# A third DMA-transposed unit in each attention layer, with two layouts on GpSimd, in a two-layer decoder trunk

## The chip, the cores and the metric

The kernel runs on one core of a Trainium2 chip. The metric is the device time of one execution in microseconds (us), lower is better. Several runs of the kernel are timed, and one more execution is recorded by the hardware profiler. In the profile PE is TensorE (PEld its weight loads), DVE is VectorE, ACT is ScalarE, POOL is GpSimd and SP is SyncE; a q behind a name (SPq) is that engine's queue of waits and DMA issues.

## What is computed

Two layers work on 512 tokens of width 1024 in float32. Each is a half-weighted SwiGLU feed-forward block, a mixing block, and a second feed-forward block. The mixing block has attention heads and a short convolution side by side:

```python
h = rms_norm(x, mix_norm[l])
z = h @ w_in[l]                      # q | k | v | conv_B | conv_C | conv_h
attn_out = sliding_window_attention(q, k, v, attn_sink[l])   # 8 heads, 2 kv heads, window 128
conv_out = short_conv(conv_B, conv_C, conv_h, conv_w[l])     # B * causal_conv3(C * h)
x = x + concat([attn_out, conv_out]) @ w_out[l]
```

In attention, a block of 128 queries sees its own 128 keys and the 128 before them (`k_band`, `v_band` below), with a bias by distance, a mask and a learned sink for each head:

```python
m = max(max(scores), sink)
p = where(mask, exp(scores - m), 0)
probs = p / (sum(p) + exp(sink - m))
out = probs @ v_band
```

## The kernel before

**Float32 by halves.** Every float32 operand is split into a high half, rounded to the format that TensorE reads (fp32r), and a low half with the remainder; a product is three matrix products (high x high, low x high, high x low). The high half of a weight (`wh`) is a cast on ScalarE, the low one (`wl`) a subtraction on VectorE (line 228). Weights come by SP from memory into buffers of the pool tag `raw`, of which there are eight; the attention tiles `p` and `vv` take buffers of the same tag.

**The mixing block.** `mix` (from about line 1482) first makes keys, values and four groups of queries. Then come twelve products of the convolution, two rounds of six (gate C twice, h twice, B twice). Attention is cut into eight units, `todo[0]` to `todo[7]`: index 0 to 3 are the four query blocks of the first key/value head, 4 to 7 those of the second. A unit holds four query heads. Index 2 is the third unit, index 3 the fourth. Units 0 and 4 are the first blocks of the sequence and have only one key block, the others two.

**Steps.** Attention is laid between the products by hand. Steps 2 to 5 follow the query groups, steps 6 to 17 the twelve products (product 9 is that of step 9). After each product `attend(step)` looks up in tables of steps which stages of which units are due:

- `scores` (table `SCORES_AT`): score products on TensorE, bias and maximum on VectorE (line 1558), exponentials on ScalarE (1575), scaling by the sum on VectorE (1583). The result `p` has queries on the partitions.
- `send` (table `SEND_AT`, step to unit): only for units 1, 3 and 5. A ScalarE copy (line 1590) lays the two 16-bit halves of all words of `p` apart into a room of the tile `crossing`, and SP issues a DMA transpose of the 16-bit rows back into the buffer of `p` (line 1592).
- `turn` (table `TURN_AT`): brings `p` to keys on the partitions. For a unit that was sent, `join` puts the turned halves together again with one ScalarE copy for each key block (line 1601). For the others TensorE transposes each head and key block into PSUM (line 1616). In both cases a ScalarE cast makes `ph` (1621) and a VectorE subtraction `pl` (1622).
- `values` (table `VALUES_AT`): two TensorE products for each key block (`ph`, line 1633; `pl`, line 1634), a ScalarE copy `ol` (1636) and two VectorE additions into `mixed[0]` (1639).

`INSIDE = (11, 4, 5)` puts the turn of unit 4 inside the product of step 11, in front of its sixth k. So `attend(10)` skips the turn that the table names for that step.

**What else runs in these steps.** In the h products (steps 8 and 9, and again 14 and 15) ScalarE makes two scaled copies, VectorE adds a tap (line 1712, both inputs in SBUF), and GpSimd does an addition and a multiplication (lines 1715 and 1716). The B products write `mixed[1]` (line 1720): its chunks 0 and 1 in steps 10 and 11, chunks 2 and 3 in steps 16 and 17.

**Order.** A scheduler at build time orders each engine's instructions, by the order of the program and by what it reckons is ready; the queues then run in that order. `issue_after` keeps the instructions of a block behind a given one on its engine. After a step, the next weights are split; if `attend` returns an instruction (the last `pl` of a turn, say), the low halves are ordered behind it. Joins are ordered behind the latest weight cast.

Of the kernel before, what the change touches and what calls it, by code (L numbers as in the profile page):

```python
# [54 lines left out]
STREAM_BACK_AT = {9: 0, 11: 1, 16: 2, 18: 3}  # L55
SCORES_AT = (5, 6, 7, 8, 9, 10, 12, 13)

SEND_AT = {7: 1, 9: 3, 11: 5}
TURN_AT = (6, 9, 8, 11, 10, 13, 14, 15)
VALUES_AT = (7, 10, 9, 12, 11, 14, 15, 16)  # L60
INSIDE = (11, 4, 5)
WARM = 3
XT_TAGS = ("sc", "aux", "aux", "mm", "sc", "sc", "aux", "aux")
# [12 lines left out]
def trunk_kernel(  # L76
# [23 lines left out]
    nc = tc.nc  # L100
# [11 lines left out]
    def g2(name, dt=F32, shape=(P, S)):  # L112
        return work.tile(list(shape), dt, tag="g2", bufs=14, name=name)

    def g8(name, dt=F32R, shape=(P, 2, 2, S)):
        return work.tile(list(shape), dt, tag="g8", bufs=4, name=name)
# [18 lines left out]
    def words(ap):  # L135

        return ap.bitcast(U16).rearrange("p (n two) -> p two n", two=2)
# [1356 lines left out]
    def mix(l, norm, after):  # L1494
        q = [None] * NH

        mixed = [g8(f"m_{l}_{j}", F32, (P, KC // 2, S)) for j in range(2)]
# [37 lines left out]
        class Unit:  # L1535
# [49 lines left out]
            def send(self):  # L1585


                self.room = crossing[:, todo.index(self) // 2 % 2, :]
                halves = self.room.bitcast(U16).rearrange("p (two n) -> p two n", two=2)
                nc.scalar.copy(halves, words(self.p.rearrange("p h k -> p (h k)")))  # L1590
                self.turned = self.p.rearrange("p h k -> p (h k)").bitcast(U16)
                nc.sync.dma_start_transpose(
                    self.turned.rearrange("p (c q) -> p c q", q=P),
                    halves.rearrange("p two n -> p (two n)"),
                )
# [11 lines left out]
            def turn(self):  # L1607

                self.pt = []
                for kb in range(self.lo // P, 2):  # L1610
                    if todo.index(self) in SEND_AT.values():
                        tp = self.join(kb)
# [30 lines left out]
        todo = [Unit(n, g) for g in range(NKV) for n in range(NT)]  # L1643
        crossing = g8(f"crossing_{l}", F32, (P, 2, 4 * 2 * P))

        def attend(step):

            done = None
            if step in SEND_AT:
                todo[SEND_AT[step]].send()  # L1650
            for at, stage in ((VALUES_AT, "values"), (TURN_AT, "turn"), (SCORES_AT, "scores")):
                if stage == "turn" and step + 1 == INSIDE[0]:
                    done = todo[VALUES_AT.index(step)].added
                    continue
                if step in at:
                    done = getattr(todo[at.index(step)], stage)() or done
            return done

        for j in range(NH // 2):
            acc = group(norm.h) if j else qacc  # L1660
            if j == 3:
                vv = take_values()
            qf = scaled(acc, f"qf_{l}_{j}", by=1.0 / 8.0)
            both = form(f"q_{l}_{j}", shape=(P, 2, S))
            qe, qo = both[:, 0, :], both[:, 1, :]
            nc.scalar.copy(qe[:HD, :], qf[:HD, :])
            nc.scalar.copy(qo[HD:, :], qf[HD:, :])
            nc.vector.tensor_sub(qe[HD:, :], qf[:HD, :], f32(qe[:HD, :]))
            nc.vector.tensor_sub(qo[:HD, :], qf[HD:, :], f32(qo[HD:, :]))
            q[2 * j], q[2 * j + 1] = qe, qo  # L1670
            attend(2 + j)
# [4 lines left out]
        step = 6  # L1676
# [9 lines left out]
        def go_on():  # L1686

            nonlocal step
            last = attend(step)
            if step == TURN_AT[-1]:  # L1690
                state["turned"] = last.ins
            step += 1
            with tc.issue_after(last.ins) if last else nullcontext():
                need_split(state["group"] - 1 + SPLIT_AHEAD + (step >= TURN_AT[-1]))

        for pair in range(2):
            cs = []
            for j in range(2):
                c = g2(f"cc_{l}_{pair}_{j}")
# [4 lines left out]
            for j in range(2):  # L1704
                c = 2 * pair + j
# [79 lines left out]
```

## Time and profile before

| what | us |
|---|---|
| median of 3 runs | 1626.99 |
| lowest and highest | 1626.08 and 1627.02 |
| the profiled execution, its own time | 1626.19 |
| its span, first to last instruction | 1624.4 |
| TensorE busy in the span | 1615.4 |
| VectorE, ScalarE, GpSimd busy | 1376.7, 1178.1, 216.5 |

The granted TensorE clock is 0.999 over the span. The steps 6 to 17 of layer 0 lie between 368 and 450 us, those of layer 1 between 1171 and 1253 us.

How to read the lines: a row of the timeline has start, duration, engine, line of the kernel, operation, output<-input, shape and count, and in brackets how long the engine was idle before it and what released it. A row of a source line has count, shortest/median/longest duration in ns, and first and last start. A row of a group has busy us and the mean of one in ns. Matrix products overlap in the pipeline, so their durations sum to more than their starts span.

### The profile page before, as it was taken

How to read it: one execution, taken by the hardware profiler on the slowest of the kernel's cores; microseconds unless marked ns; L12 is line 12 of the kernel's file. 1: busy time of each engine (PE TensorE's matmuls, PEld its weight loads, DVE VectorE, ACT ScalarE, POOL GpSimd, SP SyncE). 2: the span in 40 equal slices, each digit the busy share in tenths (PEclk: the TensorE clock that was granted, in tenths of full speed). 3: DMA queues.
4: the chain of work that ended last, by engine and by line, in shares of the span. 5: the costliest groups of instructions: out<-in, count | busy, mean ns of one | idle time of the engine just before them, and what ended most of it. 6: DMA issues, size and time to landing. Idle time of an engine off the chain costs nothing.

```text
span 1624.4 us, 21158 instructions
## 1 busy us (share of the span) xinstructions
PE 1615.4 (99%) x7571; PEld 1349.4 (83%) x7571; DVE 1376.7 (85%) x1788; ACT 1178.1 (73%) x1511; POOL 216.5 (13%) x191
## 2 busy tenths in 40 slices
PE   9999999999999999999999999999999999999998
PEld 7888888888898888888888888888888988888887
DVE  7978798988899977798998777989688998678997
ACT  6677777857766677778866777788586767878665
POOL 1211111001211111111011111110012111111121
PEclk9999999999999999999999999999999999999999
DMA  9999989822597698999767999998136978999892
GB/s 270 212 232 209 220 207 226 233 59 78 143 227 175 177 225 214 218 214 225 218 144 182 224 215 226 215 221 217 42 91 156 233 149 219 225 223 222 241 230 72
DMA packets 306031, 313.92 MB, mean 193 GB/s; under 512 B 125501, under 2 KB 188549, under 8 KB 305925
## 3 DMA queue, kind: packets, MB, share of 16 engines
q1 hardware_dynamic: 265412, 230.90, 50.1%
q0 software_dynamic: 40048, 81.27, 29.3%
q8 instruction: 59, 0.97, 0.2%
q14 instruction: 48, 0.39, 0.1%
q10 hardware_dynamic: 464, 0.40, 0.1%
HBM read 264.29 MB, written 2.10 MB: 164 GB/s over the span
## 4 chain that ended last, share of the span: by engine, by line
PE 98%; DVE 1%; DMA 0%; SPq 0%; issue 0%; ACT 0%; DVEq 0%
PE x L842 27%; PE y L842 13%; PE x_s L842 9%; PE acc L318 7%; PE acc L319 7%; PE acc L321 7%; PE w L842 7%; PE y_s L842 5%; PE x_m L827 3%; PE w_s L842 3%; PE y_m L827 1%; PE y_e L842 1%; PE acc L699 1%; PE x_e L842 1%; PE w_m L827 1%; PE sc L1555 0%
## 5 line engine op out<-in xcount | busy, mean ns | idle before, releaser
L228 DVE TENSOR_TENSOR wl<-raw,wh 128x1024 fp32r<-128x1024 f32 (+1 forms) x494 | 598.6, 1219 | 162.8 <-ACT wh L228 161.9
L228 ACT CAST wh<-raw 128x1024 fp32r<-128x1024 f32 (+1 forms) x494 | 514.1, 1044 | 304.6 <-PE x L842 92.8
L318 PE MATMUL acc<-xh,wh 128*128 128x512 f32 x392 | 153.3, 393 | 0.5 <-ACT wh L228 0.5
L319 PE MATMUL acc<-xl,wh 128*128 128x512 f32 x392 | 153.1, 391 | 0.0
L321 PE MATMUL acc<-xh,wl 128*128 128x512 f32 x384 | 149.7, 390 | 0.0
L223 POOL DMA_DIRECT2D raw<-in_ffn_wu_dram x40 | 50.6, 1272 | 381.6 <-DMA raw<-in_ffn_wu_dram 268.6
L318 PEld LDWEIGHTS acc<-xh,wh 128*128 128x128 f32 x392 | 73.8, 188 | 15.0 <-ACT wh L228 0.6
L319 PEld LDWEIGHTS acc<-xl,wh 128*128 128x128 f32 x392 | 73.7, 188 | 14.5
L321 PEld LDWEIGHTS acc<-xh,wl 128*128 128x128 f32 x384 | 72.1, 188 | 15.3
L223 POOL DMA_DIRECT2D raw<-in_ffn_wd_dram x34 | 41.0, 1218 | 272.0 <-DMA raw<-in_ffn_wd_dram 122.3
L223 POOL DMA_DIRECT2D raw<-in_ffn_wg_dram x40 | 49.1, 1237 | 201.9 <-DMA raw<-in_ffn_wu_dram 84.7
L269 DVE TENSOR_TENSOR raw<-raw,raw 128x1024 f32<-128x1024 f32 x58 | 70.5, 1220 | 1.7 <-DMA raw<-in_ffn_wu_dram 1.2
L1106 ACT COPY raw_a<-turned 128x1024 uint16<-128x1024 uint16 x48 | 63.5, 1357 | 0.0
L842 PE MATMUL x<-wl,ft1h 128*128 128x512 f32 x160 | 62.4, 390 | 0.0
L842 PE MATMUL w<-wh,fb21h 128*128 128x512 f32 x160 | 62.3, 390 | 0.0
L842 PE MATMUL y<-wh,ft3h 128*128 128x512 f32 x160 | 62.3, 390 | 0.0
L842 PE MATMUL x<-wh,ft1l 128*128 128x512 f32 x160 | 62.3, 389 | 0.0
L842 PE MATMUL x<-wl,ft2h 128*128 128x512 f32 x160 | 62.3, 389 | 0.0
L842 PE MATMUL x<-wh,ft2l 128*128 128x512 f32 x160 | 62.3, 389 | 0.0
L842 PE MATMUL x<-wh,ft1h 128*128 128x512 f32 x160 | 62.3, 389 | 0.0
L842 PE MATMUL w<-wh,fb21l 128*128 128x512 f32 x160 | 62.2, 389 | 0.0
L842 PE MATMUL y<-wh,ft3l 128*128 128x512 f32 x160 | 62.2, 389 | 0.0
(517 smaller groups left out, 4545.2 us busy)
## 6 DMA issues: line engine op xcount, KB each, us to landing
raw<-in_ffn_wu_dram SPq DMA_DIRECT2D x127, 512.0 KB, 5.6
raw<-in_ffn_wd_dram SPq DMA_DIRECT2D x105, 512.0 KB, 5.6
raw<-in_ffn_wg_dram SPq DMA_DIRECT2D x86, 512.0 KB, 5.3
raw<-in_ffn_wu_dram POOLq DMA_DIRECT2D x40, 512.0 KB, 9.1
raw<-in_ffn_wg_dram POOLq DMA_DIRECT2D x40, 512.0 KB, 6.5
raw<-in_w_in_dram SPq DMA_DIRECT2D x36, 512.0 KB, 4.0
raw<-in_ffn_wd_dram POOLq DMA_DIRECT2D x34, 512.0 KB, 8.2
raw<-in_w_out_dram SPq DMA_DIRECT2D x20, 512.0 KB, 4.6
```

What stands on the lines that cost most here:

```text
L223: nc.gpsimd.dma_start(out=r, in_=rows_of(*more), accum_op=ALU.add)
L228: return nc.scalar.copy(hi, raw), eng.tensor_sub(lo, raw, f32(hi))
L269: nc.vector.tensor_add(a11, a11, s1)
L318: nc.tensor.matmul(acc, hi[:, k, :], rhs[k][0], start=k == first, stop=False)
L319: nc.tensor.matmul(acc, hi[:, k, :], rhs[k][1], start=False, stop=False)
L321: nc.tensor.matmul(acc, lo[:, k, :], rhs[k][0], start=False, stop=k == last)
L699: nc.tensor.matmul(opening[n], (lo if part == "w" else hi)[:, k, :], xl if part == "x" else xh, start=n not in begun, stop=k == KC - 1 and ...
L827: nc.tensor.matmul(accs[c // 2][:, c % 2, :], w[:, k, cols], x_[:, 2 * h + k, :], start=start and c % 2 == 0 and h + k + i == 0, stop=h + ...
L842: nc.tensor.matmul(accs[u], x_[:, 2 * h + k, tok], w[:, k, :], start=start and h + k + i == 0, stop=h + k == 2 and i == 2, skip_group_chec ...
L1106: nc.scalar.copy(words(raws[self.b][:, c, :]), self.to[:, :, c, :])
```

## The change

Unit 2 of each layer joins units 1, 3 and 5: it is sent in step 8 and turned by DMA. Its turn moves from step 8 to step 10, its values from step 9 to step 11. The laying apart of units 2 and 3 is a GpSimd copy (`IDLE_LAYS`), that of units 1 and 5 stays on ScalarE. As a room, unit 2 uses chunks 2 and 3 of `mixed[1]`. The third edit lets two units turn in the same step, so that unit 4's turn inside product 11 can be skipped in step 10 while unit 2's is made; what the next low weights of step 10 are ordered behind stays the same (unit 1's additions).

```diff
-SEND_AT = {7: 1, 9: 3, 11: 5}
-TURN_AT = (6, 9, 8, 11, 10, 13, 14, 15)
-VALUES_AT = (7, 10, 9, 12, 11, 14, 15, 16)
+SEND_AT = {7: 1, 8: 2, 9: 3, 11: 5}
+TURN_AT = (6, 9, 10, 11, 10, 13, 14, 15)
+VALUES_AT = (7, 10, 11, 12, 11, 14, 15, 16)
+IDLE_LAYS = (2, 3)
...
-                self.room = crossing[:, todo.index(self) // 2 % 2, :]
+                n = todo.index(self)
+                self.room = crossing[:, n // 2 % 2, :]
+                if n % 2 == 0:
+                    self.room = mixed[1][:, 2:4, :].rearrange("p c s -> p (c s)")
                 halves = self.room.bitcast(U16).rearrange("p (two n) -> p two n", two=2)
-                nc.scalar.copy(halves, words(self.p.rearrange("p h k -> p (h k)")))
+                whole = words(self.p.rearrange("p h k -> p (h k)"))
+                (nc.gpsimd.tensor_copy if n in IDLE_LAYS else nc.scalar.copy)(halves, whole)
...
             for at, stage in ((VALUES_AT, "values"), (TURN_AT, "turn"), (SCORES_AT, "scores")):
-                if stage == "turn" and step + 1 == INSIDE[0]:
-                    done = todo[VALUES_AT.index(step)].added
-                    continue
-                if step in at:
-                    done = getattr(todo[at.index(step)], stage)() or done
+                for n in (n for n, when in enumerate(at) if when == step):
+                    if stage == "turn" and n == INSIDE[1]:
+                        done = todo[VALUES_AT.index(step)].added
+                    else:
+                        done = getattr(todo[n], stage)() or done
             return done
```

## The prediction

> **What bounds the kernel now.** I read the page's busy times and chain of waits first, then the stretch of layer 0 in which attention runs, then single instructions there.
>
> ```profile
> PE 1615.4 (99%) x7571; PEld 1349.4 (83%) x7571; DVE 1376.7 (85%) x1788; ACT 1178.1 (73%) x1511; POOL 216.5 (13%) x191
> ...
> PE 98%; DVE 1%; DMA 0%; SPq 0%; issue 0%; ACT 0%; DVEq 0%
> ```
>
> TensorE is busy for 99% of the span and makes 98% of the chain that ended last. So an edit pays what it takes off TensorE, and costs what it makes TensorE wait; work on other engines counts only where TensorE ends up waiting for it. The next view is the stretch from 388 to 405 us (steps 8 to 11 of layer 0). Its columns after the stretch are its length and the busy time of PE, PEld, DVE, ACT and POOL, each with a count, then the granted clock, the DMA share and GB/s.
>
> ```profile
> 388.00:405.00 17.00, 17.00 (x91) 14.15 (x90) 15.52 (x45) 15.62 (x31) 5.51 (x4) 1.00 0.36 94
> ```
>
> TensorE has no gap here, but VectorE is free for only 17.00 - 15.52 = 1.48 us and ScalarE for 1.38 us, while GpSimd is free for 11.5 us. The change puts its new work into this tight stretch. In all of both layers' attention TensorE waits for one thing only, the low halves pl (time and times):
>
> ```profile
>   PEld o L1634: 1.4, 5
> ```
>
> **Removed: the transposes.** The third unit (index 2) gives up eight TensorE transposes in each layer, 16 of these 64:
>
> ```profile
> L1616 PE MATMUL pt<-ident,p x64: 270/272/319, 376.5 to 1242.0; 128*128 128x128 f32 x64
> ```
>
> A burst of eight is put in the middle of a weight product, so its price can be read from the starts of its neighbours:
>
> ```profile
> 389.57 0.40 PE L318 MATMUL acc<-xh,wh 128*128 128x512 f32 x1
> 389.81 1.12 PE L1616 MATMUL pt<-ident,p 128*128 128x128 f32 x8
> 390.69 0.48 PE L319 MATMUL acc<-xl,wh 128*128 128x512 f32 x1
> 391.01 0.39 PE L321 MATMUL acc<-xh,wl 128*128 128x512 f32 x1
> 391.23 0.40 PE L318 MATMUL acc<-xh,wh 128*128 128x512 f32 x1
> 391.46 0.39 PE L319 MATMUL acc<-xl,wh 128*128 128x512 f32 x1
> ...
> 1192.35 0.40 PE L318 MATMUL acc<-xh,wh 128*128 128x512 f32 x1
> ...
> 1193.78 0.39 PE L321 MATMUL acc<-xh,wl 128*128 128x512 f32 x1
> ```
>
> Two products take 391.46 - 391.01 = 0.45 us. From 389.57 to 391.01 two products and the burst took 1.44 us, so the burst costs 0.99 us; in layer 1 it is 1193.78 - 1192.35 - 0.45 = 0.98 us. Together -1.97 us. Note that 16 x 272 ns would be 4.35 us: the durations overlap, and the starts tell the price. If against these starts each transpose were worth its whole duration, the time would fall by 4.35 us to 1622.6; I give that 0.02. The Trainium skill, "TensorE: Matmul & The Clock Gate", section "Part 4: PE-mode transpose", puts a transpose at about 275 ns in one kernel's context. The row's 272 ns agrees as a duration, not as a price: by the page the gain would be 4.4 us, by the starts it is 1.97 us.
>
> **Added to ScalarE and the DMA queue.**
>
> ```profile
> L1590 ACT COPY crossing<-p x6: 1897/1897/1902, 383.0 to 1216.2; 128x2048 uint16<-128x2048 uint16 x6
> ...
> L1601 ACT COPY crossing<-p x12: 1339/1359/1373, 388.9 to 1223.0; 128x1024 uint16<-128x1024 uint16 x12
> ...
> L1621 ACT CAST ph<-crossing x12: 602/618/622, 399.0 to 1228.3; 128x512 fp32r<-128x512 f32 x12
> ...
> L1592 SPq DMA_TRANSPOSE p<-crossing x6: 1567/1613/1627, 385.0 to 1218.1; - x6
> ...
> DMA to landing us min/median/max: 3.6/3.7/5.2
> ```
>
> In each layer ScalarE gains two joins of unit 2 (2 x 1.36 = 2.72 us) and loses unit 3's laying apart (1.90 us), which goes to GpSimd: +0.82 us; the two casts ph stay but move from step 8 to step 10. SP gains one transpose: 1.6 us of issue and 3.7 us to landing. Unit 2's data are due only in step 11, some 20 us after its p is ready, so its chain of laying, transpose, joins, casts (3.1 + 3.7 + 2.7 + 1.2 = 10.7 us) is covered. If ScalarE had no gaps, the price would be 0.82 us a layer; I take 0, because the 1.90 us leave just where the joins arrive.
>
> The tile p of unit 2 now stays in its buffer until its joins. Before, the next weight load took that buffer at once:
>
> ```profile
> 390.96 0.37 SPq L210 DMA_DIRECT2D raw<-in_w_in_dram  x1
> ...
> 412.48 1.05 ACT L228 CAST wh<-raw 128x1024 fp32r<-128x1024 f32 x1
> ```
>
> By the order of loads and casts this weight is cast at 412.48, 21.5 us later. One buffer fewer for 13 to 17 us pushes it back by less than that: 0, and microsecond for microsecond beyond it.
>
> **Added to GpSimd.** Two copies of 128x2048 uint16 in each layer, of which this trace has none on that engine. The nearest rows:
>
> ```profile
> L173 POOL CAST ones_r<-ones 128x128 fp32r<-128x128 f32 x1 | 0.3, 288 | 0.0
> ...
> L1716 POOL TENSOR_TENSOR cc<-cc,inv x8: 1289/1463/2153, 393.7 to 1247.5; 128x512 f32<-128x512 f32 x8
> ```
>
> At the cast's whole 288 ns for 128 elements 2048 take 4.6 us, most likely too much, as a start-up is in it; the fastest case is ScalarE's 1.9 us for the same copy; the slowest is the slowest addition's 2153 / 512 = 4.2 ns an element, 8.6 us. I take 3.1 us, between the first two. GpSimd has the time. What counts is VectorE, which slows beside it:
>
> ```profile
> 399.82 1.29 POOL L1715 TENSOR_TENSOR cc<-cc,tap 128x511 f32<-128x511 f32 x1 [4.79 <-issue]
> 401.19 1.63 POOL L1716 TENSOR_TENSOR cc<-cc,inv 128x512 f32<-128x512 f32 x1
> ...
> 400.48 1.18 DVE L1622 TENSOR_TENSOR pl<-crossing,ph 128x512 fp32r<-128x512 f32 x1
> ...
> 402.40 0.97 DVE L1622 TENSOR_TENSOR pl<-crossing,ph 128x512 fp32r<-128x512 f32 x1
> ...
> 403.37 1.21 DVE L228 TENSOR_TENSOR wl<-raw,wh 128x1024 fp32r<-128x1024 f32 x1
> ...
> L1622 DVE TENSOR_TENSOR pl<-pt,ph x16: 680/692/694, 378.0 to 1247.4; 128x512 fp32r<-128x512 f32 x16
> L1622 DVE TENSOR_TENSOR pl<-crossing,ph x12: 659/694/1181, 400.5 to 1229.6; 128x512 fp32r<-128x512 f32 x12
> ```
>
> The first pl took 1.18 us for 0.69 and ended 0.55 us after GpSimd's first instruction (399.82 + 1.29 = 401.11); the second took 0.97 and ended 0.55 us after GpSimd's next one (402.82). Both look as if they stood until GpSimd was done. So a VectorE instruction with two SBUF inputs may be held to the end of a laying apart. The Trainium skill, "SBUF — State Buffer", section "Who interferes with whom", says that such an instruction contends with a GpSimd one that reads SBUF; by its summary the second to issue fully blocks. The trace agrees, with the two ends 0.55 us behind GpSimd's.
>
> Now what is late next. VectorE must finish the low weights of product 11 (403.37 + 1.21 = 404.58) before TensorE's first use, the first row below; the other rows are unit 2's value products, which move from step 9 to step 11, and the VectorE additions behind them.
>
> ```profile
> 405.19 0.39 PE L321 MATMUL acc<-xh,wl 128*128 128x512 f32 x1
> ...
> 395.32 0.39 PE L1633 MATMUL o<-ph,vv 128*128 128x512 f32 x1
> ...
> 396.23 0.22 PE L1554 MATMUL sc<-kh,q 128*128 128x128 f32 x1
> ...
> L1639 DVE TENSOR_TENSOR m<-o,ol x32: 386/416/419, 383.3 to 1251.9; 64x256 f32<-64x256 f32 x32
> ```
>
> Slack before: 0.61 us. TensorE comes earlier by the burst, 0.99, and the moved value products, 0.91: 1.90 us. VectorE loses two pl (1.38) and two additions (0.83): 2.21 us earlier. Slack after without any hold: 0.61 + 2.21 - 1.90 = 0.92 us. The holds, from when their data are ready (the scaled p, then the tap):
>
> ```profile
> 389.19 1.13 DVE L1583 TENSOR_SCALAR p<-p,sums 128x256 f32<-128x256 f32 x4
> ...
> 391.48 0.75 DVE L1712 SCALAR_TENSOR_TENSOR tap<-ch,par,tap 128x510 f32<-128x510 f32 x1 [0.34 <-ACT tap L1711]
> ...
> 397.90 1.13 DVE L1583 TENSOR_SCALAR p<-p,sums 128x256 f32<-128x256 f32 x4
> 398.95 0.74 DVE L1712 SCALAR_TENSOR_TENSOR tap<-ch,par,tap 128x510 f32<-128x510 f32 x1
> ```
>
> Unit 2's laying would run from 390.32 to 393.4 and hold the tap due at 391.48 for 1.9 us; unit 3's from 399.03 to 402.1 and hold the pl due at 400.48 for 1.6, where 0.6 were lost already. In all 2.9 us more; the slack (0.92) and VectorE's gaps (1.48) cover 2.4. Uncovered: 0.5 us a layer if every hold is full, 0 if none is. I take half: +0.5 us for both layers.
>
> **The sum.** -1.97 + 0.5 = -1.5 us. The profiled execution took 1626.19 us (span 1624.4 and 1.8 around it) and would take 1624.7; the median of the runs shown, 1626.99, lies 0.8 above it and would become **1625.5**.
>
> **Rivals.**
>
> *The holds decide (0.27).* If VectorE's gaps can't be used, because they lie elsewhere than the holds, 2.9 - 0.92 = 2.0 us of wait a layer stand against 0.98 saved: +1.0 a layer, **1629.0**. For it: the stretch is the tightest of the layer, and the pl are the one thing that TensorE already waits for. Against it: low weights may be made earlier, since step 8 no longer orders them behind unit 2's pl.
>
> *Unit 3 comes late through GpSimd's queue (0.20).* Its laying is ready at 399.03, and the addition of the convolution at 398.95 + 0.74 = 399.69. If the program has the two additions in front, laying begins at 402.8, ends at 405.9, and lands at 409.6.
>
> ```profile
> 405.88 2.57 ACT L1601 COPY crossing<-p 128x1024 uint16<-128x1024 uint16 x2
> ...
> 408.78 0.59 ACT L1621 CAST ph<-pt 128x512 fp32r<-128x512 f32 x1 [0.33 <-PE pt L1616]
> ...
> 410.67 0.39 PE L1633 MATMUL o<-ph,vv 128*128 128x512 f32 x1
> ```
>
> ScalarE stands at unit 3's joins, queued behind which is unit 4's ph: joins to 412.2, ph to 412.8, pl to 413.5. TensorE wants that pl at 410.67 + 0.23 - 0.99 = 409.9: it waits 3.6 us. Net 2 x (3.6 - 0.98) = +5.2: **1632.2**. It decides from about 1.3 us of lateness on (0.33 of gap plus the 0.98 saved). For it: only 0.66 us lie between the two; against: the laying is ready first, and the joins may be ordered later.
>
> *The old waits go too (0.05).* With ol and ph of unit 2 out of step 9, unit 1's pl come earlier and the 1.4 us of wait vanish, with no hold: -3.4, **1623.6**.
>
> *It does not act (0.04).* The scheduler fills the freed places with other waits: **1627.0**. Against it: the transposes are certainly gone.
>
> **How the numbers follow.** Forecast 0.42 (its own range 1624.2 to 1626.6), holds 0.27, late unit 3 0.20, old waits 0.05, whole durations 0.02, nothing 0.04. A measurement of this kernel tells about 0.2%, 3.25 us, from no change. Faster than that (below 1623.7): 0.05 + 0.02 = 0.07. Slower (above 1630.2): 0.20. Within: 0.73. The range, 1623.6 to 1631.0, reaches from the old waits' end past the holds; it leaves out most of the late unit 3 and of the whole durations.
>
> **What would show it.** Right: 48 transposes at L1616, and product 9 without the 0.99 us; a GpSimd copy near 3 us; TensorE's waits for pl below 2.4 us. The holds: pl, tap or low weights well over 0.7 and 1.2 us beside a copy, and TensorE waiting at product 11. The late unit: GpSimd's additions ahead of unit 3's copy and ScalarE waiting for a transpose. Wrong altogether: weights waiting for their loads, or TensorE gaps outside steps 8 to 12.

## The result and the profile after

| what | before | after |
|---|---|---|
| median of 5 runs each, us | 1626.93 | 1632.72 |
| lowest and highest, us | 1626.08 and 1627.02 | 1631.61 and 1634.13 |
| span of the profiled execution, us | 1624.4 | 1630.9 |
| granted TensorE clock over the span | 0.999 | 0.996 |

The ratio is 1.004, with a 95% interval of 1.0029 to 1.005. The change made the kernel 5.8 us slower. The forecast was 1625.5 us in a range up to 1631.0, so it had the wrong sign and the range did not hold the time. Four of the five executions after have a granted clock of 0.996 or 0.997; the fifth has 0.999, as before the change, and took 1631.61 us.

The busy times and the chain of waits of the changed kernel:

```profile
PE 1616.8 (99%) x7555; PEld 1350.1 (83%) x7555; DVE 1386.6 (85%) x1788; ACT 1179.3 (72%) x1513; POOL 224.5 (14%) x195
...
PE 93%; DVE 4%; DMA 1%; ACT 1%; issue 1%; SPq 0%; POOL 0%; DVEq 0%; ACTq 0%; POOLq 0%
```

TensorE has 16 matrix instructions fewer and is busy for 1.4 us longer. VectorE's share of the chain that ended last went from 1% to 4%. The rows of the changed lines (count, shortest/median/longest in ns, first and last start) show that the edit is there:

```profile
L1621 PE MATMUL pt<-ident,p x48: 270/272/316, 376.4 to 1248.0; 128*128 128x128 f32 x48
...
L1595 POOL COPY m<-p x2: 2262/2272/2282, 391.4 to 1197.0; 128x2048 uint16<-128x2048 uint16 x2
L1595 POOL COPY crossing<-p x2: 1889/1889/1889, 397.9 to 1203.6; 128x2048 uint16<-128x2048 uint16 x2
```

There are 48 transposes, not 64, and four GpSimd copies of 1.9 and 2.3 us. (Lines are later by 1 up to the edit and by 5 behind it: pl is L1627, the value products are L1638 and L1639.) TensorE's waits in attention (time, times and the longest, in us):

```profile
PEld o L1639 <- DVE pl L1627: 6.2, 5, 2.7
...
PE o L1639 <- DVE pl L1627: 4.6, 2, 2.3
```

It is the same wait as before, 1.4 us then, and 4.6 us of it are two waits of 2.3 us, one a layer. The two stretches of layer 0 that follow each other, first the second of them before and then both after (columns as in the prediction):

```profile
405.00:420.00 15.00, 15.00 (x73) 12.55 (x72) 13.13 (x41) 12.12 (x24) 0.00 (x0) 1.00 0.47 119
```

```profile
388.00:405.00 17.00, 14.69 (x72) 11.96 (x71) 16.31 (x39) 15.05 (x36) 9.56 (x6) 0.98 0.39 94
405.00:420.00 15.00, 15.00 (x67) 12.57 (x66) 12.86 (x38) 13.05 (x24) 0.00 (x0) 0.91 0.38 112
```

TensorE has a gap of 2.3 us, and behind it the granted clock is 0.91: it is busy for all 15 us, but with fewer instructions done (67 for 73). The instructions around the gap, TensorE's first, then GpSimd's, then VectorE's:

```profile
401.32 0.39 PE L1638 MATMUL o<-ph,vv 128*128 128x512 f32 x1
404.02 0.61 PE L1639 MATMUL o<-pl,vv 128*128 128x512 f32 x1 [2.31 <-DVE pl L1627]
404.43 0.42 PE L1555 MATMUL sc<-kh,q 128*128 128x256 f32 x1
404.65 0.42 PE L1556 MATMUL sc<-kl,q 128*128 128x256 f32 x1
...
406.57 0.63 PE L320 MATMUL acc<-xl,wh 128*128 128x512 f32 x1
407.00 0.63 PE L322 MATMUL acc<-xh,wl 128*128 128x512 f32 x1
...
407.78 0.39 PE L320 MATMUL acc<-xl,wh 128*128 128x512 f32 x1
...
419.62 0.39 PE L1638 MATMUL o<-ph,vv 128*128 128x512 f32 x1
...
1225.31 0.39 PE L1638 MATMUL o<-ph,vv 128*128 128x512 f32 x1
...
397.89 1.89 POOL L1595 COPY crossing<-p 128x2048 uint16<-128x2048 uint16 x1 [1.65 <-DVE p L1584]
400.47 1.59 POOL L1720 TENSOR_TENSOR cc<-cc,tap 128x511 f32<-128x511 f32 x1 [0.69 <-DVE tap L1717]
402.14 1.28 POOL L1721 TENSOR_TENSOR cc<-cc,inv 128x512 f32<-128x512 f32 x1
...
398.28 2.05 DVE L1717 SCALAR_TENSOR_TENSOR tap<-ch,par,tap 128x510 f32<-128x510 f32 x1
...
401.23 0.86 DVE L1570 TENSOR_SCALAR nm<-mx 128x4 f32<-128x4 f32 x1
...
402.20 1.77 DVE L1627 TENSOR_TENSOR pl<-crossing,ph 128x512 fp32r<-128x512 f32 x1
```

The same places before:

```profile
403.08 0.39 PE L1633 MATMUL o<-ph,vv 128*128 128x512 f32 x1
403.43 0.50 PE L1634 MATMUL o<-pl,vv 128*128 128x512 f32 x1
...
403.30 0.16 DVE L1569 TENSOR_SCALAR nm<-mx 128x4 f32<-128x4 f32 x1
...
416.57 0.39 PE L1633 MATMUL o<-ph,vv 128*128 128x512 f32 x1
...
1219.30 0.39 PE L1633 MATMUL o<-ph,vv 128*128 128x512 f32 x1
```

How these rows are read. Unit 1's last value product (step 10) needs the second pl. TensorE is at that place at 401.32, against 403.08 before: 1.76 us early, from 0.98 us of transposes that are gone and 0.91 us of unit 2's value products that now come later, less some 0.1 us that it already loses at the first pl. VectorE is not early. GpSimd's copy of unit 3 ends at 399.78 and the tap at 400.33, 0.55 us behind it; the tap should take 0.75 us and took 2.05. That delays GpSimd's addition, which waits for the tap. Before, unit 4's nm (four numbers on a partition) stood behind the second pl, at 403.30; the scheduler now has it ahead. There it stands until the addition's end at 402.06, and the second pl until the end of GpSimd's product (403.42), again 0.55 us behind. So pl is done at 403.97, and was at 403.37.

Then TensorE starts score products every 0.21 us, not every 0.12, and weight products every 0.43 us, not 0.23, until about 407.6. Before, the third product of product 11 (405.19, a row of the prediction) came 1.76 us after the product that waits; after, 407.00 - 404.02 = 2.98 us, and from there to 407.78 another 0.3 us go: about 1.5 us are lost to the clock in this execution.

By layer: -0.98 (transposes), +2.35 (the step from 401.32 to 404.02 is 2.70 us, and was 0.35), +1.5 (clock) = +2.9 us. The next landmark, unit 3's first value product, came 419.62 - 416.57 = 3.05 us later, and that of layer 1 6.01 us later (1225.31 against 1219.30). That is nearly all of the span's 6.5 us. The split between wait and clock is that of the traced execution: the one with a clock of 0.999 was only 1.1 us below the median, and no trace of it was kept.

### The profile page after: what moved, and what is told of

The parts are those of the page before. It is cut to its first block, busy times and chain, and to the rows that moved or that the text cites. A ratio compares the mean times of both kernels' runs of the same rounds, so it can differ in the third digit from the quotient of the medians.

```text
span 1630.9 us, 21137 instructions
## 1 busy us (share of the span) xinstructions
PE 1616.8 (99%) x7555; PEld 1350.1 (83%) x7555; DVE 1386.6 (85%) x1788; ACT 1179.3 (72%) x1513; POOL 224.5 (14%) x195
## 4 chain that ended last, share of the span: by engine, by line
PE 93%; DVE 4%; DMA 1%; ACT 1%; issue 1%; SPq 0%; POOL 0%; DVEq 0%; ACTq 0%; POOLq 0%
PE x L843 27%; PE y L843 13%; PE x_s L843 9%; PE w L843 7%; PE acc L319 6%; PE acc L320 6%; PE acc L322 6%; PE y_s L843 5%; PE w_s L843 3%; PE x_m L828 2%; PE y_m L828 1%; PE y_e L843 1%; PE acc L700 1%; DVE wl L229 1%; PE x_e L843 1%
## 5 line engine op out<-in xcount | busy, mean ns | idle before, releaser
L843 PE MATMUL w<-wl,fb21h 128*128 128x512 f32 x160 | 62.2, 389 | 0.0
```

Of the source, the lines that this page charges most:

```text
L843: nc.tensor.matmul(accs[u], x_[:, 2 * h + k, tok], w[:, k, :], start=start and h + k + i == 0, stop=h + k == 2 and i == 2, skip_group_chec ...
```

## The experiments

The trace says where the time goes. Open were three things: whether the copies on GpSimd, the moved value products or the order of VectorE make TensorE wait, whether the saving could have shown at all, and what ScalarE would do instead. Times are medians; the kernel before stood at 1626.1 to 1626.6 us beside these runs. "Lost to starts" below is the net sum, over steps 8 to 17 of one layer (388 to 452 us in layer 0), by which the starts of TensorE's instructions lie further apart than at full rate (0.227 us for 512 columns, 0.117 for 256, 0.113 for 128); it is 0.6 to 0.8 us before and 4.5 us after.

### Which engine lays the halves apart

Both copies on ScalarE, `IDLE_LAYS = ()`:

```diff
-IDLE_LAYS = (2, 3)
+IDLE_LAYS = ()
```

> Both layings apart go back to ScalarE; unit 2 is still turned by DMA. Theory A (VectorE's pl of unit 1 are held by GpSimd instructions, whichever these are, and TensorE waits and then runs at a lower granted clock): the convolution's two GpSimd instructions alone still hold the second pl, TensorE's longest wait at unit 1's value products is 1 to 2 us instead of 2.3, the time 1628 to 1631. Theory B (only the GpSimd copies are to blame): no wait over 0.4 us, 1625. Theory C (ScalarE is late with the joins): ScalarE has 3.8 us more in each layer, so the time is over 1633.

Measured: 1633.09 us, ratio 1.0039 (1.0025 to 1.0053). GpSimd's copies are gone and the time is as long, as theory C had it. Only unit 2 on GpSimd, `IDLE_LAYS = (2,)`:

> Only unit 2 is laid apart by GpSimd, unit 3 by ScalarE as before. Theory A: the tap of product 9 is no longer held, the convolution's GpSimd pair comes earlier, but it still holds nm, es and pl of unit 1, which stand behind each other: wait 1.5 to 2 us, 1629 to 1632. Theory B with unit 3's copy as the culprit: no wait, 1625. Theory C: 1633 or more.

Measured: 1629.0 us, ratio 1.0015 (1.0006 to 1.0025), the lower end of theory A; the wait at step 10 is 1.31 us, less than it had. Only unit 3 on GpSimd, `IDLE_LAYS = (3,)`:

> The changed kernel with unit 2's halves laid by ScalarE and unit 3's by GpSimd, the fourth case beside both, unit 2 alone and none. Theory: unit 3's copy holds the tap and the pair behind it as in the changed kernel, and ScalarE carries one more copy: 1632.5 to 1635. Rival (ScalarE's load is what costs): between 1629.0 and 1632.7.

Measured: 1631.25 us, ratio 1.0028 (1.0017 to 1.0039). It lies between, as the rival had it, not above the changed kernel. The stretch from 388 to 420 us of layer 0 (columns as above), first before, then both copies on ScalarE, then unit 2 on GpSimd alone:

```profile
388.00:420.00 32.00, 32.00 (x162) 26.70 (x161) 28.65 (x85) 27.74 (x53) 5.51 (x4) 1.00 0.41 106
```

```profile
388.00:420.00 32.00, 30.34 (x147) 24.53 (x146) 24.48 (x75) 31.95 (x63) 5.52 (x4) 1.00 0.41 106
```

```profile
388.00:420.00 32.00, 30.59 (x149) 24.76 (x148) 28.96 (x77) 31.22 (x61) 7.38 (x5) 1.00 0.43 112
```

With both copies ScalarE is busy for 31.95 of 32 us. TensorE then waits mostly for pl (3.8 us in both layers), and VectorE, busy for only 24.48 us, waits for ScalarE in turn (0.69 us for unit 1's second ph, 2.52 us for es, the exponential of a sink). With unit 2 alone on GpSimd, ScalarE is busy for 31.22 us. So the copies have no good place: on ScalarE they fill it, on GpSimd they hold VectorE. Unit 2's copy is better on GpSimd (1633.1 to 1629.0); with that done, unit 3's is better left on ScalarE (1629.0 against 1632.7).

### The copy of unit 3 by itself

The kernel before, with one edit:

```diff
-                nc.scalar.copy(halves, words(self.p.rearrange("p h k -> p (h k)")))
+                (nc.gpsimd.tensor_copy if todo.index(self) == 3 else nc.scalar.copy)(
+                    halves, words(self.p.rearrange("p h k -> p (h k)"))
+                )
```

> The kernel before, with another part alone: unit 3's halves laid apart by GpSimd, not ScalarE; everything else stays. Theory (the moved products): the copy holds the tap and, through the pair of the convolution behind it, unit 1's second subtraction, some 0.7 us per layer late, and TensorE is on time there: +1.0 to +1.6 us in all, 1627.4 to 1628.0. Rival (GpSimd's copies decide all): most of the 6.3 us, 1630 or more. If ScalarE was late too and gains by it: 1626.4.

Measured: 1629.89 us, ratio 1.002 (1.0011 to 1.0029): +3.3 us, twice the upper end of what the theory had, and just below where its rival began. Its timeline:

```profile
399.13 2.34 POOL L1590 COPY crossing<-p 128x2048 uint16<-128x2048 uint16 x1 [4.06 <-DVE p L1583]
401.43 1.73 POOL L1717 TENSOR_TENSOR cc<-cc,tap 128x511 f32<-128x511 f32 x1
...
400.51 1.51 DVE L1624 TENSOR_TENSOR pl<-crossing,ph 128x512 fp32r<-128x512 f32 x1
...
402.21 1.50 DVE L1624 TENSOR_TENSOR pl<-crossing,ph 128x512 fp32r<-128x512 f32 x1
...
404.18 1.76 DVE L228 TENSOR_TENSOR wl<-raw,wh 128x1024 fp32r<-128x1024 f32 x1
...
405.99 0.50 PE L321 MATMUL acc<-xh,wl 128*128 128x512 f32 x1 [0.31 <-DVE wl L228]
```

Both pl end 0.55 us behind a GpSimd instruction (402.02 and 401.47; 403.71 and 403.16), and then TensorE waits for the low weights of product 11: the rival of the prediction in which the holds decide, at its place. This part of the change costs by itself.

### The moved value products by themselves

The kernel before, with unit 2's value products at step 11 (and the loop of the change's third edit, so that the values of two units can be due in one step):

```diff
-VALUES_AT = (7, 10, 9, 12, 11, 14, 15, 16)
+VALUES_AT = (7, 10, 11, 12, 11, 14, 15, 16)
```

> The kernel before, with one part of the change alone: unit 2's value products stand at step 11 and no longer at step 9; all its transposes stay on TensorE and no copy goes to GpSimd. Theory (the moved products): these four products, 0.91 us, stood ahead of unit 1's second pair of products and covered VectorE's subtraction; without them TensorE reaches that pair 0.91 us early, waits, and does the 0.91 us later, so +0.8 to +0.9 us per layer, 1627.9 to 1628.3 us. If VectorE gains as much because unit 2's addition now comes behind the subtraction: 1626.4. Rival (GpSimd's copies and what they hold up decide all): 1626.4, no wait at that pair longer than before's.

Measured: 1628.66 us, ratio 1.0012 (1.0003 to 1.0021): +2.1 us, a little above the theory's +1.6 to +1.8. TensorE, VectorE and ScalarE at step 10:

```profile
402.47 0.49 PE L1633 MATMUL o<-ph,vv 128*128 128x512 f32 x1
403.51 0.50 PE L1634 MATMUL o<-pl,vv 128*128 128x512 f32 x1 [0.55 <-DVE pl L1622]
...
402.45 1.01 DVE L1622 TENSOR_TENSOR pl<-crossing,ph 128x512 fp32r<-128x512 f32 x1 [0.70 <-ACT ph L1621]
...
399.05 1.05 ACT L228 CAST wh<-raw 128x1024 fp32r<-128x1024 f32 x1
```

The product starts at 403.51, and at 403.43 before: TensorE was early and got nothing for it, and does the 0.91 us afterwards. The second pl itself waited 0.70 us for ScalarE's ph. But the order differs here too: the scheduler had put a weight cast of 1.05 us ahead of that ph, which before came behind it (ph at 401.33, casts from 401.85). So the run does not show by itself that ScalarE and VectorE could not have been earlier.

### Unit 1 turned or used at another step

Unit 1 turned in step 8, to have its pl early:

```diff
-TURN_AT = (6, 9, 10, 11, 10, 13, 14, 15)
+TURN_AT = (6, 8, 10, 11, 10, 13, 14, 15)
...
-                        done = getattr(todo[n], stage)() or done
+                        last = getattr(todo[n], stage)()
+                        done = None if step == 8 else last or done
```

> The changed kernel with unit 1's turn moved from step 9 to step 8 (the place that unit 2 left), and the low weights of step 8 not ordered behind it; both copies stay on GpSimd. Theory A: unit 1's pl are made before product 10 ends whatever holds them, TensorE does not wait for them and keeps its clock, and the whole saving of the transposes shows: 1625.0 (1624.4 to 1626). Theory C or late data of units 2 and 3: the time stays near 1632.

Measured: 1632.81 us, ratio 1.0038 (1.0025 to 1.0051). The wait at step 10 is gone, and waits for the scaled p, ph and pl of other units stand in steps 11 and 12 in its place (4.2 us lost to starts in each layer). The theory that had 1625.0 missed, and the time is near 1632, as its rival had it. Unit 1's value products moved to step 11 instead, with both copies on GpSimd, and then with unit 2's alone:

```diff
-VALUES_AT = (7, 10, 11, 12, 11, 14, 15, 16)
+VALUES_AT = (7, 11, 11, 12, 11, 14, 15, 16)
...
-                        done = todo[VALUES_AT.index(step)].added
+                        done = todo[1].last
```

> The changed kernel with unit 1's value products at step 11, together with unit 2's and unit 4's, and no longer at step 10; both copies stay on GpSimd. Theory (TensorE reaches unit 1's second pair 1.9 us ahead of VectorE): the wait of 2.3 us and the slow stretch behind it are gone, 1624.5 to 1627 us; a new wait at step 11 of up to 0.6 us per layer would make the upper end. Rival (VectorE held by GpSimd's copies is late whatever stands there, and the next thing that it makes is waited for instead): 1630 to 1633.

> As the run with unit 1's products at step 11, but only unit 2's halves laid by GpSimd and unit 3's by ScalarE. Theory: 1624.5 to 1626.5 us against 1629.0 with the products at step 10. Rival (ScalarE's and VectorE's lateness is only passed on): 1628 to 1630.

Measured: 1633.99 us, ratio 1.0045 (1.0033 to 1.0058), and 1630.82 us, ratio 1.0028 (1.0017 to 1.004). Both theories missed. The rivals had the mechanism, but both times lie 0.8 to 1.0 us above their ranges (up to 1633 and 1630). TensorE in the second of the two:

```profile
403.11 0.40 PE L320 MATMUL acc<-xl,wh 128*128 128x512 f32 x1
405.38 0.50 PE L322 MATMUL acc<-xh,wl 128*128 128x512 f32 x1 [1.87 <-DVE wl L229]
405.71 0.39 PE L319 MATMUL acc<-xh,wh 128*128 128x512 f32 x1
405.94 0.53 PE L320 MATMUL acc<-xl,wh 128*128 128x512 f32 x1
406.28 0.63 PE L322 MATMUL acc<-xh,wl 128*128 128x512 f32 x1
```

TensorE no longer waits for pl but for the low weights that VectorE makes behind it (the other run's wait is 2.71 us). This trace is of the slowest of six executions (1633.91 us, granted clock 0.997); two others kept 0.999 and took 1629.88 and 1630.12 us. The lateness is VectorE's, and is passed on to whatever it makes next. Score products put ahead of the wait, with unit 2's copy alone on GpSimd:

```diff
+            if step == 10:
+                todo[5].scores()
+                stages.pop()
```

> Only unit 2's halves by GpSimd, nothing left out; at step 10 unit 5's eight score products (0.95 us) stand ahead of unit 1's value products, not behind them. Theory (work ahead of the wait covers it): the wait of 1.5 us falls by up to 0.95 us per layer, 1627.0 to 1627.8 us against 1629.0. Rival (VectorE's lateness is only passed on, to the low half of product 11): 1628.6 to 1630.

Measured: 1630.68 us, ratio 1.003 (1.0018 to 1.0041), slower than without (1629.0) and above the ranges of theory and rival. The wait for pl fell to 0.4 us, and in step 11 TensorE waited 1.4 us for ScalarE's ph instead, not for the low weights that the rival named.

### The wait filled

Ten products with zeros ahead of unit 1's value products, to keep the clock up:

```diff
+                if todo.index(self) == 1:
+                    spin(10, o)
```

> The changed kernel with ten matrix products of zeros (10 x 0.227 = 2.3 us) put on TensorE in front of unit 1's value products; they are overwritten. They fill the 2.3 us in which TensorE waits. If the slow products after the wait come from the wait (theory A's second half), they are gone and the time falls by 1.7 us a layer to 1629.3. If the slow products have another cause, the time stays at 1632.7; if the wait is moved and not filled, it rises by up to 4.6 us to 1637.

Measured: 1636.84 us, ratio 1.0062 (1.0047 to 1.0077). The granted clock was 1.00 from 388 to 420 us, but the products took 2 us, and a wait of 1.6 us came at step 11. Nothing about the clock's share follows from it.

### VectorE less held

GpSimd's two operations on the second group of the convolution (addition and product) are left out, so that nothing holds VectorE there, in the kernel before, in the changed one and in the one with unit 2 alone. The convolution's second group is then not finished.

```diff
+                if c != 1:
+                    nc.gpsimd.tensor_add(y[:, 1:], y[:, 1:], tap[:, 1:])
+                    nc.gpsimd.tensor_mul(y, y, norm.inv)
-                nc.gpsimd.tensor_add(y[:, 1:], y[:, 1:], tap[:, 1:])
-                nc.gpsimd.tensor_mul(y, y, norm.inv)
```

> The kernel before without GpSimd's two operations on the second group of the convolution (the addition of the tap and the product with the norm's inverse, 1.29 and 1.63 us in each layer), so that nothing of GpSimd holds VectorE while it makes unit 1's subtractions; it is the base for the next two. Both theories: TensorE waited only 0.1 us per layer there, so 1625.9 to 1626.6 us, next to no gain.

> The changed kernel without the same two operations; unit 3's copy of 1.89 us still holds the tap. Theory (TensorE comes 1.9 us early to a subtraction that VectorE's queue cannot make earlier, and GpSimd's pair behind the copy holds it): the second subtraction ends 1.5 to 1.9 us earlier, the wait falls from 2.3 to 0.4 to 0.9 us, the slow stretch goes: 1625.4 to 1627.2. Rival (another chain, ScalarE's or the DMA's, ends as late): 1630 or more.

> Only unit 2's halves by GpSimd, unit 3's by ScalarE, and the same two operations left out. Theory: the subtraction ends some 1.6 us earlier than in the run with unit 2 alone, at the time at which TensorE comes; the whole saving of 1.97 us shows against the base without the pair: 1624.2 to 1625.4. Rival: still 1628 to 1629, something else is late there.

Measured: 1626.16 (ratio 0.9998, 0.9989 to 1.0007), 1629.23 (1.0017, 1.0008 to 1.0025) and 1628.19 us (1.0011, 1.0002 to 1.002). The base is as fast as before. The changed kernel gains 3.5 us: its wait at step 10 falls from 2.3 to 0.5 us and the clock stays at 1.00, as expected; the one with unit 2 alone gains 0.8 us. But the times stay above the theory's, because waits come at steps 11 and 12. In the run with unit 2 alone:

```profile
410.58 0.51 PE L1638 MATMUL o<-ph,vv 128*128 128x512 f32 x1 [0.17 <-ACT ph L1626]
411.31 0.50 PE L1639 MATMUL o<-pl,vv 128*128 128x512 f32 x1 [0.22 <-DVE pl L1627]
```

First ScalarE, then VectorE is late for unit 4. Its transposes are done by 407.4, but ScalarE casts its ph only at 409.94, behind unit 2's second join and both its ph, the joins of unit 3 and a weight cast. Unit 2's joins are what the change added there.

### The saving alone

The kernel before without unit 2's transposes: its parts are split from p as it lies, unturned; no copy, no DMA, and the value products stay.

```diff
+                    elif todo.index(self) == 2:
+                        tp = self.p[:, :, kb * P : (kb + 1) * P]
```

> The kernel before with unit 2's sixteen transposes left out: its parts are split straight from the probabilities, not turned; no copy, no DMA, and its value products stay at step 9. It is the saving alone. Theory (VectorE's second subtraction for unit 1 decides step 10, so TensorE's time is worth nothing ahead of it): the wait there grows by what is saved, 1625.9 to 1626.6 us. Rival (the saving is real and only the copies and the moved products lose it): 1624.2 to 1624.8.

> The same, and GpSimd's two operations on the second group of the convolution left out too, as in the base without them (1626.2). Theory: VectorE's subtraction is no longer held by 0.5 us twice, so part of the saving shows: 1624.4 to 1625.4. Rival (saving real in any case): 1624.2, with no difference from the run that keeps the two operations.

Measured: 1627.41 us, ratio 1.0004 (0.9996 to 1.0013), and without GpSimd's two operations 1627.49 us, ratio 1.0007 (0.9998 to 1.0016). Nothing is gained; the second expectation, that part of the saving would then show, missed. Both traces also show another order on VectorE and ScalarE: the scheduler had put nm and a weight cast ahead of unit 1's parts. So the orders were held as before the change and the run repeated (the edit in part):

```diff
+                pin = {3: 2, 4: 1}.get(todo.index(self))
+                with tc.issue_after(todo[pin].last.ins) if pin else nullcontext():
+                    nc.vector.tensor_scalar_mul(nm, mx, -1.0)
...
+                    if todo.index(self) == 1 and kb == 0:
+                        self.first = last
+                        with tc.issue_after(self.cast.ins):
+                            todo[3].send()
```

> Unit 2's transposes left out of the kernel before once more, and the orders of VectorE and ScalarE held as they were (unit 3's and unit 4's nm behind the subtractions, unit 3's copy between the two casts of unit 1, the next weight casts behind them); without that the scheduler had put a weight cast and nm ahead. Theory (VectorE and ScalarE decide steps 9 and 10 in any order): 1625.9 to 1626.6 us. Rival (their chain follows TensorE's products, and only the new order lost the saving): the full 1.97 us, 1624.2 to 1624.9.

Measured: 1626.68 us, ratio 1.0003 (0.9994 to 1.0012). The saving of 1.97 us would be a ratio of 0.9988, which lies outside all three intervals. The trace of the last run:

```profile
402.66 0.48 PE L1644 MATMUL o<-ph,vv 128*128 128x512 f32 x1
404.02 0.50 PE L1645 MATMUL o<-pl,vv 128*128 128x512 f32 x1 [0.89 <-DVE pl L1628]
...
401.08 1.19 DVE L1628 TENSOR_TENSOR pl<-crossing,ph 128x512 fp32r<-128x512 f32 x1
...
403.01 0.96 DVE L1628 TENSOR_TENSOR pl<-crossing,ph 128x512 fp32r<-128x512 f32 x1
...
394.58 1.25 DVE L1573 TENSOR_SCALAR nm<-mx 128x4 f32<-128x4 f32 x1
...
394.19 1.62 POOL L1729 TENSOR_TENSOR cc<-cc,inv 128x512 f32<-128x512 f32 x1
```

Nothing of the copies or of the moved products is in this kernel, and still TensorE gives the time back at the same product: the second pl ends at 403.97, not earlier than before (403.37). In this run VectorE's chain through steps 8 to 10 does not become shorter when TensorE does. One difference remains, and it counts: unit 2's own subtractions here read two SBUF tiles, as they do in the changed kernel, while before one input was in PSUM. Beside them GpSimd's first product took 1.62 us and ended at 395.81 (1.29 us and 395.03 before), unit 3's nm stood until then (1.25 us for 0.66), and the low weights behind it began 0.77 us late. The other two runs have much the same times there. So all three leave-out runs make VectorE late themselves, by about as much as the second pl is late (0.60 us here). Without that the pl would, by these rows, be done about when it was before, and the saving would still not show; that is an argument, and no run has it.

### The order in the changed kernel

Unit 4's nm ordered behind unit 1's second pl, nothing left out:

```diff
+                pin = {4: 1}.get(todo.index(self))
+                with tc.issue_after(todo[pin].last.ins) if pin else nullcontext():
+                    nc.vector.tensor_scalar_mul(nm, mx, -1.0)
```

> The changed kernel with unit 4's nm ordered behind unit 1's second subtraction, as the kernel before has it; nothing left out. Theory (order and holds): nm no longer stands 0.86 us for GpSimd ahead of the subtraction, which is held to the end of GpSimd's addition and not of the product behind it, 1.36 us earlier; the wait falls to about 1 us and the slow stretch goes: 1626.6 to 1629. Rival (the lateness is only passed on, to the low half of product 11 or unit 2's parts): 1630 to 1632.7.

Measured: 1629.5 us, ratio 1.0021 (1.0012 to 1.003): 3.2 us faster than the changed kernel, 0.5 us outside what the theory gave.

```profile
401.27 1.50 DVE L1629 TENSOR_TENSOR pl<-crossing,ph 128x512 fp32r<-128x512 f32 x1
...
402.82 0.50 PE L1642 MATMUL o<-pl,vv 128*128 128x512 f32 x1 [0.95 <-DVE pl L1629]
...
405.12 0.50 PE L322 MATMUL acc<-xh,wl 128*128 128x512 f32 x1 [0.38 <-DVE wl L229]
```

The second pl ends at 402.77, 1.2 us earlier, the wait is 0.95 us, and the clock is not lowered. Part is passed on to the low weights (0.38 us) and to unit 4's pl in step 11 (0.64 us), as the rival said.

None of the versions beats the kernel before. Its own loss to starts is some 0.7 us a layer, so hardly any waiting was there to win back.

## Why the prediction was wrong

**What bounds the kernel.** The page's 99% and 98% for TensorE were read as "an edit pays what it takes off TensorE". That step failed first. In steps 8 to 10 VectorE, with 15.52 of 17 us, and ScalarE, with 15.62, are nearly as full as TensorE, and VectorE arrives together with it: the second pl is done at 403.37, and TensorE could have used it from 403.31 (403.08 + 0.23). The wait for pl was short because TensorE was just as late. The prediction quoted both numbers and used them for the cost of additions only, not for the worth of the saving.

**-1.97 us for the transposes.** The size of the burst was right: TensorE is early by just that and by the moved products. Its worth was not: left out alone, it gained nothing in three runs (+0.6 to +1.0 us against the kernel before, not clear of no change). Why it gained nothing is in part argued, since leaving it out also made VectorE late there.

**The GpSimd copy at 3.1 us.** It took 1.89 us, and 2.26 us beside other VectorE work, at the lower bound of 1.9.

**The holds.** The rule was right: the tap and the second pl ended 0.55 us behind GpSimd's instructions. The Trainium skill, "SBUF — State Buffer", section "Who interferes with whom", has a rule for tensor_scalar as well: it can contend in its 2-port modes. The trace agrees that it is held: nm, a TENSOR_SCALAR of four numbers, stood for 0.86 us until GpSimd's addition was done (402.09 and 402.06); in which mode it ran no row tells. The prediction had no hold on nm, and no term for the order of VectorE: with nm back behind the second pl the changed kernel is 3.2 us faster.

**The slack of 0.92 us.** This step failed second. It was taken at the low weights of product 11, the last thing VectorE makes, although the same pages showed that TensorE already waited for pl, 1.76 us earlier. TensorE's 1.90 us ahead were counted, but at pl there was no slack of 0.61 us to begin with, and VectorE's 2.21 us less of work were not a lead: the run with the moved products alone shows the product that needs the second pl at the same time as before. The half of the holds that was to vanish in VectorE's gaps did not: in the changed kernel these lie ahead of 396 us, where VectorE waits for others, and from there to 404 us it is busy for 7.90 of 8 us.

**The clock.** No term stood for what a wait does to TensorE afterwards. In the trace it was 1.5 us a layer, three times what the holds were to cost at their fullest (0.5 us a layer). By the granted clocks it does not come in every execution, and the one with a clock of 0.999 is still 4.7 us above the kernel before.

**ScalarE and the buffer, both at 0.** In the changed kernel this held: TensorE waits for no ph, and for a high half of a weight no longer than before (0.5 us, once). It held with both copies on GpSimd; with unit 2's copy on ScalarE, TensorE waits 2.3 us for ph in both layers together, and with both there ScalarE is full.

**The rivals.** The holds that decide (1629.0) had the mechanism; that it strikes at pl and brings the clock down was missing. The late unit 3 had the number (1632.2) by chance: GpSimd copied unit 3 at 397.89, ahead of the addition at 400.47, and the delay was VectorE's. The old waits did not go; they grew.

The sum with the measured terms, by layer: 0.98 saved against 2.35 of wait and 1.5 of clock. Of the wait, 1.76 us are TensorE's lead, made of the saved and the moved products, and 0.60 us VectorE's lateness (403.97 against 403.37). So the saving is inside the wait, and what is left as loss is the moved 0.91, the 0.60 and the clock: 3.0 us. The moved products and the clock had no term of their own in the prediction.

## What to carry to other kernels

Time that is taken off the busiest engine counts only up to the next place where it meets another engine, so measure the lead there: leave the work out altogether in one run, and see in its trace whether leaving it out changed anything else. If nothing is gained even so, moving the work is unlikely to gain. Work that stood ahead of a wait is cover; moved behind it, it costs its whole length again. A scheduler may also answer an edit with another order, so look at the order of the engine that is late. And the wait of 2.3 us cost more than half as much again here, in the traced execution, through the clock, so price what comes after a wait too.

## What the runs showed of the hardware

**The clock can fall after short waits.** A wait of 2.31 us was followed by 3.4 us at half rate (0.43 us for 0.227). By the profile's idle times in layer 0, waits of 0.95, 1.24, 1.31 and 1.62 us in four of the traced executions had no slow stretch behind them, and waits of 1.87, 2.31 and 2.71 us had. In the run of 1.87 us the slow products began 0.6 us later in layer 0 and at once in layer 1. This is no sharp limit: the trace with 1.87 us is of the slowest of six executions, and two others of the same kernel kept a clock of 0.999. The Trainium skill, "TensorE: Matmul & The Clock Gate", section "Why this matters for your kernels", asks for no idle gaps above about 3 us. By that rule the wait of 2.31 us would have cost 2.31 us alone; here slow stretches came behind shorter waits, from 1.87 us on.

**A GpSimd copy of 128x2048 uint16 costs what ScalarE's does.** It took 1.89 us on GpSimd (2.26 to 2.34 us beside other work of VectorE) and 1.90 us on ScalarE; what differs is whom it holds.

**A short VectorE instruction is held as long as a long one.** nm, of four numbers on a partition, took 0.16 us where GpSimd was idle (403.30 before) and 0.66 to 1.33 us where it waited for GpSimd's instruction to end, and what is queued behind it moves with it.
